# Row dot products and softmax: x of a batch loaded as one 8 MB transfer instead of two of 4 MB

## Chip, cores and metric

One Trainium2 chip, one core. The metric is the device time of one execution in microseconds (us). Executions of the kernel before ran from 325.33 to 326.04 us (0.2%), so a difference of 1 us (0.3%) needs several runs, and one of 0.5 us needs the trace as well. Every run also has a span: the time from the program's first instruction to the end of its last. It is about 2 us shorter than the device time.

## What the kernel must compute

```python
B, N, D = 8, 4096, 512          # x, y: float32 [B, N, D]
gram = np.matmul(x, y.transpose(0, 2, 1))
diag = np.diagonal(gram, axis1=1, axis2=2)      # diag[b, n] = sum over d of x[b, n, d] * y[b, n, d]
diag = diag - diag.max(axis=-1, keepdims=True)
exp = np.exp(diag)
out = exp / exp.sum(axis=-1, keepdims=True)     # [8, 4096]
```

Only the diagonal is needed, so the work is 32,768 dot products of 512 elements and a softmax per batch. Each input byte is used once: x and y are 134.22 MB, and all of it must come from memory.

Of the kernel before, what the change touches and what calls it, by code (L numbers as in the profile page):

```python
# [1 line left out]

# [5 lines left out]


@with_exitstack
def kernel(
    ctx: ExitStack,
    tc: tile.TileContext,
    x: bass.AP,
    y: bass.AP,
    out: bass.AP,
):
    nc = tc.nc
    f32 = mybir.dt.float32  # L20
    B, N, D = x.shape
    P = nc.NUM_PARTITIONS
    R = N // P
    H = R // 2


    xv = x.rearrange("b (p r) d -> b p r d", p=P)
    yv = y.rearrange("b (p r) d -> b p r d", p=P)
    ov = out.rearrange("b (p r) -> b p r", p=P)

    io = ctx.enter_context(tc.tile_pool(name="io", bufs=3))
    persist = ctx.enter_context(tc.tile_pool(name="persist", bufs=1))
    sm = ctx.enter_context(tc.tile_pool(name="sm", bufs=2))

    diag = persist.tile([P, B * R], f32, name="diag")
    res = persist.tile([P, B * R], f32, name="res")

    def load(b, r0, parts):
        xt = io.tile([P, H, D], f32, tag="xt", name="xt")
        yt = io.tile([P, H, D], f32, tag="yt", name="yt")  # L40
        o = 0
        for n in parts:
            nc.sync.dma_start(out=xt[:, o : o + n, :], in_=xv[b, :, r0 + o : r0 + o + n, :])  # L43
            nc.sync.dma_start(out=yt[:, o : o + n, :], in_=yv[b, :, r0 + o : r0 + o + n, :])
            o += n
        return xt, yt

    def dots(b, r0, xt, yt):
        for k in range(H):
            c = b * R + r0 + k  # L50
            nc.vector.scalar_tensor_tensor(  # L51
                out=xt[:, k, :],
                in0=xt[:, k, :],
                scalar=1.0,
                in1=yt[:, k, :],
                op0=mybir.AluOpType.mult,
                op1=mybir.AluOpType.mult,
                accum_out=diag[:, c : c + 1],
            )

    def softmax(b):
        db = diag[:, b * R : (b + 1) * R]
        rb = res[:, b * R : (b + 1) * R]
        mxp = sm.tile([P, 1], f32, tag="mxp", name="mxp")
        nc.vector.tensor_reduce(out=mxp, in_=db, axis=mybir.AxisListType.X, op=mybir.AluOpType.max)  # L65
        mx = sm.tile([P, 1], f32, tag="mx", name="mx")
        nc.gpsimd.partition_all_reduce(out_ap=mx, in_ap=mxp, channels=P, reduce_op=bass_isa.ReduceOp.max)  # L67
        nmx = sm.tile([P, 1], f32, tag="nmx", name="nmx")
        nc.vector.tensor_single_scalar(out=nmx, in_=mx, scalar=-1.0, op=mybir.AluOpType.mult)  # L69
        sump = sm.tile([P, 1], f32, tag="sump", name="sump")  # L70
        nc.scalar.activation(  # L71
            out=rb, in_=db, func=mybir.ActivationFunctionType.Exp,
            bias=nmx, scale=1.0, accum_out=sump,
        )
        ssum = sm.tile([P, 1], f32, tag="ssum", name="ssum")
        nc.gpsimd.partition_all_reduce(out_ap=ssum, in_ap=sump, channels=P, reduce_op=bass_isa.ReduceOp.add)  # L76
        rc = sm.tile([P, 1], f32, tag="rc", name="rc")
        nc.vector.reciprocal(out=rc, in_=ssum)  # L78
        nc.vector.tensor_single_scalar(out=rb, in_=rb, scalar=rc, op=mybir.AluOpType.mult)  # L79
        nc.scalar.dma_start(out=ov[b], in_=rb)  # L80

    for b in range(B):
        for h in range(2):
            last = b == B - 1 and h == 1
            parts = [8, 4, 2, 1, 1] if last else [H]
            xt, yt = load(b, h * H, parts)
            dots(b, h * H, xt, yt)
        softmax(b)


# [1 line left out]
_INS = ['x', 'y']  # L92
_OUTS = [((8, 4096), 'float32')]


# [23 lines left out]
```

## The kernel before

Partition p holds rows 32p to 32p+31 of a batch, so its rows are one contiguous run of 64 KB in memory. A batch is worked in two halves of 16 rows. Each half has an x tile and a y tile of 32 KB per partition, in three buffers each (192 KB per partition in all).

```python
R = N // P        # 32 rows per partition
H = R // 2        # 16
io = ctx.enter_context(tc.tile_pool(name="io", bufs=3))
...
def load(b, r0, parts):
    xt = io.tile([P, H, D], f32, tag="xt", name="xt")
    yt = io.tile([P, H, D], f32, tag="yt", name="yt")
    o = 0
    for n in parts:
        nc.sync.dma_start(out=xt[:, o : o + n, :], in_=xv[b, :, r0 + o : r0 + o + n, :])
        nc.sync.dma_start(out=yt[:, o : o + n, :], in_=yv[b, :, r0 + o : r0 + o + n, :])
        o += n
    return xt, yt

def dots(b, r0, xt, yt):
    for k in range(H):
        c = b * R + r0 + k
        nc.vector.scalar_tensor_tensor(out=xt[:, k, :], in0=xt[:, k, :], scalar=1.0, in1=yt[:, k, :],
            op0=mult, op1=mult, accum_out=diag[:, c : c + 1])
...                      # softmax(b): two reductions over partitions, one exp, one store
for b in range(B):
    for h in range(2):
        last = b == B - 1 and h == 1
        parts = [8, 4, 2, 1, 1] if last else [H]
        xt, yt = load(b, h * H, parts)
        dots(b, h * H, xt, yt)
    softmax(b)
```

The last half comes in pieces of 8, 4, 2, 1 and 1 rows, so that little work is left when the last byte lands.

## Time and profile before

| | before |
|---|---|
| time, median | 325.55 us (3 runs, 325.4 to 325.62) |
| span in the profile | 323.8 us |
| load packets, time per DMA engine (sum over packet records / 16) | 313.0 us |
| 32 KB packet | 1213 ns (median) |
| last load landed | 318.36 us |
| middle of its 16 parts landed; 15 of the 16 landed | 314.60 us; 314.83 us |

Lines of the page of the kernel before: busy time of the engines, and part 3, which has for each DMA queue its packets, megabytes and the share of the span of 16 DMA engines that its packets took. The load queue fills 96.6% of the DMA engines' time; VectorE (DVE) only half of its own. "q14 instruction" is the queue that fetches the engines' instructions, five packets within the span.

```profile
span 323.8 us, 727 instructions
DVE 164.4 (51%) x544; ACT 4.6 (1%) x17; POOL 6.1 (2%) x20
...
q1 hardware_dynamic: 5760, 134.22, 96.6%
q10 hardware_dynamic: 1152, 0.13, 0.3%
q14 instruction: 5, 0.04, 0.0%
```

The same kernel by stretches of time. After the stretch come the busy times of the engines, the granted clock, the mean share of the DMA engines that was busy, and the rate. From 22 to 306 us the DMA engines have no free time (share 1.00, 431 GB/s). From 306 to 318 us the share falls to 0.70 although the last load lands only at 318.36 us: most DMA engines are done and wait for one.

```profile
core 0: us, DVE busy (x) ACT busy (x) POOL busy (x), PEclk, DMA share, GB/s
22.00:306.00 284.00, 151.07 (x501) 2.90 (x14) 5.13 (x14) 1.00 1.00 431
306.00:318.00 12.00, 11.87 (x40) 0.00 (x0) 0.00 (x0) 1.00 0.70 279
```

The groups of the page (line, engine, operation, count, busy us, mean ns, then the idle time of the engine before them and what ended it), and the end of the chain of waits (start, length, what). All waits of VectorE's products are for loads of y (in the softmaxes it waits another 11.9 us for GpSimd); after the last landing there are about 5.5 us of products, softmax and store.

```profile
L51 DVE SCALAR_TENSOR_TENSOR xt<-xt,yt 128x512 f32<-128x512 f32 x256 | 158.3, 687 | 144.1 <-DMA yt<-in_y_dram 144.1
```

```profile
269.00 39.28 DMA yt<-in_y_dram
308.28 0.01 issue
308.30 10.06 DMA yt<-in_y_dram
...
318.45 0.71 DVE xt L51 x2
...
321.31 0.24 DVE res L79
```

### The profile page before, as it was taken

The page shows a single profiled execution, that of the slowest core. Times are in us where ns is not written, and L with a number is a line of the kernel's source. Part 1 is how long each engine was busy: PE and PEld are TensorE (multiplying, and loading weights), DVE is VectorE, ACT ScalarE, POOL GpSimd, SP SyncE. Part 2 cuts the span into 40 slices and gives each one's busy share as a digit, 9 for nine tenths or more (in the row PEclk, how much of TensorE's full clock was granted, in tenths as well). Part 3 has the DMA queues.
Part 4 walks back from the last instruction along what each step waited for, and adds up shares of the span by engine and source line. Part 5 has one row for each costly group of instructions (what it writes and reads, how often), then busy time and mean ns, then how long its engine had stood idle before and what let it go on. Part 6 is the DMA issues. An engine that isn't in the chain of part 4 may idle for free.

```text
span 323.8 us, 727 instructions
## 1 busy us (share of the span) xinstructions
DVE 164.4 (51%) x544; ACT 4.6 (1%) x17; POOL 6.1 (2%) x20
## 2 busy tenths in 40 slices
DVE  0019075290944709256191742908348091571994
ACT  1000000000000000000000000000000000000000
POOL 0000000000000000000000000000000000000000
DMA  8999999999999999999999999999999999999980
GB/s 324 453 401 441 453 410 429 455 409 433 449 397 451 445 401 446 450 398 449 449 397 450 452 393 453 445 397 455 445 397 453 446 394 453 445 397 425 429 319 10
DMA packets 6917, 134.39 MB, mean 415 GB/s; under 512 B 1792, under 2 KB 1792, under 8 KB 2560
## 3 DMA queue, kind: packets, MB, share of 16 engines
q1 hardware_dynamic: 5760, 134.22, 96.6%
q10 hardware_dynamic: 1152, 0.13, 0.3%
q14 instruction: 5, 0.04, 0.0%
HBM read 134.22 MB, written 0.13 MB: 415 GB/s over the span
## 4 chain that ended last, share of the span: by engine, by line
DMA 82%; DVE 16%; issue 1%; SPq 0%; POOLq 0%; POOL 0%; DVEq 0%
DMA yt<-in_y_dram 82%; DVE xt L51 16%; SPq L43 0%; DVE mxp L65 0%; POOLq L114 0%; POOL mx L67 0%; DVE res L79 0%; DVE rc L78 0%; DVEq L51 0%; DVEq L79 0%; POOLq L67 0%
## 5 line engine op out<-in xcount | busy, mean ns | idle before, releaser
L51 DVE SCALAR_TENSOR_TENSOR xt<-xt,yt 128x512 f32<-128x512 f32 x256 | 158.3, 687 | 144.1 <-DMA yt<-in_y_dram 144.1
L51 DVE DVE_READ_ACCUMULATOR xt<-xt,yt 128x1 f32 x256 | 21.1, 82 | 0.0
L67 POOL PARTITION_ALL_REDUCE mx<-mxp x8 | 2.8, 350 | 308.9 <-DVE mxp L65 308.9
L71 ACT ACTIVATE res<-diag,nmx 128x32 f32<-128x32 f32 x8 | 2.6, 321 | 315.2 <-DVE nmx L69 315.2
L78 DVE RECIPROCAL rc<-ssum 128x1 f32<-128x1 f32 x8 | 1.3, 164 | 7.6 <-POOL ssum L76 7.6
L69 DVE TENSOR_SCALAR nmx<-mx 128x1 f32<-128x1 f32 x8 | 1.2, 154 | 4.3 <-POOL mx L67 4.3
L76 POOL PARTITION_ALL_REDUCE ssum<-sump x8 | 3.1, 383 | 5.8 <-ACT res L71 5.8
L79 DVE TENSOR_SCALAR res<-res,rc 128x32 f32<-128x32 f32 x8 | 1.9, 241 | 0.9
L65 DVE TENSOR_REDUCE mxp<-diag 128x1 f32<-128x32 f32 x8 | 1.5, 186 | 0.3
L71 ACT ACTIVATION_READ_ACCUMULATOR res<-diag,nmx 128x1 f32 x8 | 1.5, 186 | 0.0
L71 ACT ACT_TABLE_LOAD x1 | 1.3, 1283 | 0.7 <-PEq L103 0.7
L103 POOL MEMSET const-float32-0.0<- 128x1 f32 x1 | 0.1, 98 | 0.2 <-issue 0.2
L103 POOL MEMSET const-bfloat16-1.0<- 128x1 bf16 x1 | 0.1, 102 | 0.0
L103 POOL MEMSET const-uint8-127<- 128x1 uint8 x1 | 0.1, 101 | 0.0
L103 POOL MEMSET const-float32-1.0<- 128x1 f32 x1 | 0.1, 98 | 0.0
## 6 DMA issues: line engine op xcount, KB each, us to landing
xt<-in_x_dram SPq DMA_DIRECT2D x15, 4096.0 KB, 39.6
yt<-in_y_dram SPq DMA_DIRECT2D x15, 4096.0 KB, 48.9
xt<-in_x_dram SPq DMA_DIRECT2D x1, 2048.0 KB, 34.7
yt<-in_y_dram SPq DMA_DIRECT2D x1, 2048.0 KB, 39.3
xt<-in_x_dram SPq DMA_DIRECT2D x1, 1024.0 KB, 41.3
yt<-in_y_dram SPq DMA_DIRECT2D x1, 1024.0 KB, 43.4
xt<-in_x_dram SPq DMA_DIRECT2D x1, 512.0 KB, 35.5
yt<-in_y_dram SPq DMA_DIRECT2D x1, 512.0 KB, 27.0
```

The source lines that it names most:

```text
L51: nc.vector.scalar_tensor_tensor(out=xt[:, k, :], in0=xt[:, k, :], scalar=1.0, in1=yt[:, k, :], op0=mybir.AluOpType.mult, op1=mybir.AluOpT ...
L65: nc.vector.tensor_reduce(out=mxp, in_=db, axis=mybir.AxisListType.X, op=mybir.AluOpType.max)
L67: nc.gpsimd.partition_all_reduce(out_ap=mx, in_ap=mxp, channels=P, reduce_op=bass_isa.ReduceOp.max)
L69: nc.vector.tensor_single_scalar(out=nmx, in_=mx, scalar=-1.0, op=mybir.AluOpType.mult)
L71: nc.scalar.activation(out=rb, in_=db, func=mybir.ActivationFunctionType.Exp, bias=nmx, scale=1.0, accum_out=sump,)
L76: nc.gpsimd.partition_all_reduce(out_ap=ssum, in_ap=sump, channels=P, reduce_op=bass_isa.ReduceOp.add)
L78: nc.vector.reciprocal(out=rc, in_=ssum)
L79: nc.vector.tensor_single_scalar(out=rb, in_=rb, scalar=rc, op=mybir.AluOpType.mult)
L103: nc = _bacc.Bacc("TRN2", target_bir_lowering=False, num_devices=1)
```

## The change

The intent: larger transfers and longer runs. x of a whole batch comes in one 8 MB load (64 KB per partition, two buffers), y in two halves (32 KB per partition, two buffers), again 192 KB. The products are written over y instead of x. The last batch keeps halves and pieces.

```diff
-    io = ctx.enter_context(tc.tile_pool(name="io", bufs=3))
+    io = ctx.enter_context(tc.tile_pool(name="io", bufs=2))
...
+    def load_x(b, xt, r0, n):
+        nc.sync.dma_start(out=xt[:, r0 : r0 + n, :], in_=xv[b, :, r0 : r0 + n, :])
+    def load_y(b, yt, r0, o, n):
+        nc.sync.dma_start(out=yt[:, o : o + n, :], in_=yv[b, :, r0 + o : r0 + o + n, :])
...
-                out=xt[:, k, :],
-                in0=xt[:, k, :],
+                out=yt[:, k, :],
+                in0=xt[:, r0 + k, :],
...
     for b in range(B):
+        last = b == B - 1
+        xt = io.tile([P, R, D], f32, tag="xt", name="xt")
+        if not last:
+            load_x(b, xt, 0, R)
         for h in range(2):
-            last = b == B - 1 and h == 1
-            parts = [8, 4, 2, 1, 1] if last else [H]
-            xt, yt = load(b, h * H, parts)
+            yt = io.tile([P, H, D], f32, tag="yt", name="yt")
+            o = 0
+            for n in [8, 4, 2, 1, 1] if last and h == 1 else [H]:
+                if last:
+                    load_x(b, xt, h * H + o, n)
+                load_y(b, yt, h * H, o, n)
+                o += n
             dots(b, h * H, xt, yt)
```

More of the change, by code (lines that the diff above doesn't have):

```diff
@@ L36 @@
     res = persist.tile([P, B * R], f32, name="res")
-    def load(b, r0, parts):
-        xt = io.tile([P, H, D], f32, tag="xt", name="xt")
-        yt = io.tile([P, H, D], f32, tag="yt", name="yt")
-        o = 0
-        for n in parts:
-            nc.sync.dma_start(out=xt[:, o : o + n, :], in_=xv[b, :, r0 + o : r0 + o + n, :])
-            nc.sync.dma_start(out=yt[:, o : o + n, :], in_=yv[b, :, r0 + o : r0 + o + n, :])
-            o += n
-        return xt, yt
+    def load_x(b, xt, r0, n):
+        nc.sync.dma_start(out=xt[:, r0 : r0 + n, :], in_=xv[b, :, r0 : r0 + n, :])
+    def load_y(b, yt, r0, o, n):
+        nc.sync.dma_start(out=yt[:, o : o + n, :], in_=yv[b, :, r0 + o : r0 + o + n, :])
     def dots(b, r0, xt, yt):
```

## The prediction

> **What bounds the kernel now.** The DMA engines. The page gives 134.22 MB on the load queue, 96.6% of 16 engines' span of 323.8 us; the table by stretch of time gives DMA share 1.00 and 431 GB/s from 22 to 306 us. The trace's packet records show 1213 ns (median) per 32 KB packet, 432 GB/s for 16 engines. The Trainium skill (DMA: Bandwidth & Descriptors, "Where 436 GB/s comes from") puts the ceiling at 435 GB/s; this trace agrees. VectorE is busy 51%; its waits are all for y loads (144.1 us). A load lands 39 to 49 us after its issue, while one 4 MB load takes 9.7 us (landings at 12.9, 22.6, 32.3, 42.0), so the queue is never empty.
>
> The span: 1.74 us to the first packet; 313.0 us of load packets per engine; 0.9 us of output packets; then one engine finishes late. The 16 landings of the last load spread over 3.84 us, 15 of them close together. The late engine falls back about 1 us at each of four instruction fetches on queue 14 (8 KB, at 47, 125, 186 and 263 us), about every 130 VectorE instructions. The same page ("Queues, rings and completion order") calls row 14 the runtime's, refill among its uses. From the last landing (318.36 us) 5.4 us of products, softmax and store follow.
>
> **What the change does.**
> - Bytes: unchanged. This is the bound.
> - Packets: in 7 of 8 batches two 32 KB runs of x become one of 64 KB, if one packet may carry that. Packets of 2, 4, 8, 16, 32 KB take 86, 160, 312, 611, 1213 ns: 602 ns per 16 KB plus 9 ns. Seven batches x 128 packets fewer are 56 per engine: 0.5 us. If the run is cut into 32 KB packets, nothing.
> - DMAs: 7 fewer, each one completion packet of 9 ns per engine: 0.06 us.
> - VectorE: the same 256 products (687 ns, 613 ns apart), in place in y instead of x; about 7 fewer semaphore waits. Off the critical path; the four fetches stay.
> - Buffers: the same 192 KB per partition. A y half is issued when the products of the same half of the batch before are done, about 10.4 us after that half landed. By then the queue holds at least 17 us more (rest of y, 19.4 us of x): no starvation. The lead was about 28 us.
> - The last batch: the same halves and pieces, so the tail of 5.4 us stays, and the wait for the late engine.
>
> **On the critical path:** only 0.5 to 0.6 us of packet overhead. Larger transfers buy almost nothing, because 32 KB packets already pay under 1% each.
>
> **Prediction:** 325.0 us (325.55 - 0.55), 80% range 323.9 to 326.2. Chances: faster by over 2% 0.01, within 2% 0.98, slower by over 2% 0.01.
>
> **What would show it.** Right: load packets of 64 KB near 2417 ns; about 896 fewer packets; DMA share 1.00 through the middle; no gap between loads; the last landing about 0.5 us earlier, its spread still near 4 us; tail 5.4 us. Wrong: 64 KB packets slower or faster than twice 1213 ns; gaps where y waits for VectorE; another count or cost of queue 14 fetches.
>
> **What would make it wrong.** A fetch could cost the late engine more when it meets a 64 KB packet (up to 1 us for each of four); or the fetches cost less or fall differently, and the late engine catches up (up to 3.7 us less). A starved queue would need VectorE or the issue to lag by 17 us.

## The result

| | before | after |
|---|---|---|
| time, median of 4 runs | 325.52 us | 325.14 us |
| range | 325.4 to 325.62 | 325.1 to 325.49 |
| ratio, 95% interval | | 0.9991 [0.9974, 1.0008] |

A ratio is the mean time of one kernel's fast runs over the mean of the other's in the same rounds, so it is not quite the ratio of the medians quoted. The interval holds 1.

The spans are sharper than the times. Over nine runs of the changed kernel (here and in after_again) they are 323.0 to 323.5 us, over 34 runs of the kernel before in all rounds with experiments 323.6 to 324.3 us: no overlap.

The page after, the same lines. 1008 packets fewer are on the load queue: 896 of them because two runs of 32 KB became one of 64 KB, and 112 completion packets of the 7 loads that are gone (16 each). The share of the DMA engines' time is the same 96.6% of a span that is 0.7 us shorter.

```profile
span 323.1 us, 714 instructions
DVE 163.9 (51%) x544; ACT 4.6 (1%) x17; POOL 6.1 (2%) x20
...
q1 hardware_dynamic: 4752, 134.22, 96.6%
q10 hardware_dynamic: 1152, 0.13, 0.3%
q14 instruction: 4, 0.03, 0.0%
```

By stretches of time: still 1.00 through the middle, still a fall before 318 us.

```profile
core 0: us, DVE busy (x) ACT busy (x) POOL busy (x), PEclk, DMA share, GB/s
22.00:306.00 284.00, 151.40 (x503) 2.90 (x14) 5.16 (x14) 1.00 1.00 432
306.00:318.00 12.00, 11.42 (x37) 0.00 (x0) 0.00 (x0) 1.00 0.65 258
```

VectorE's group, and the end of the chain. VectorE waits as long as before (143.8 us), and the last landing is at 317.58 us instead of 318.36.

```profile
L47 DVE SCALAR_TENSOR_TENSOR yt<-xt,yt 128x512 f32<-128x512 f32 x256 | 157.9, 687 | 143.8 <-DMA yt<-in_y_dram 143.8
```

```profile
288.19 19.32 DMA yt<-in_y_dram
307.51 0.02 issue
307.52 10.06 DMA yt<-in_y_dram
...
317.68 0.71 DVE yt L47 x2
...
320.54 0.24 DVE res L75
```

From the packet records: a 64 KB packet takes 2419 ns (median), a 32 KB packet 1213 ns, so the rate is the same.

**The late DMA engine.** Each load lands in 16 parts, read here as one per DMA engine. These are landing times of six loads in each kernel, read from the trace (us: first part, middle part, last part, spread):

```
before  51.26  51.51  52.52  1.27      after   70.52  70.83  71.56  1.05
        80.48  80.68  81.71  1.22             109.33 109.62 110.36  1.03
       148.65 148.77 150.71  2.06             148.13 148.43 150.16  2.03
       197.26 197.35 200.28  3.02             254.78 255.14 257.84  3.06
       265.31 265.41 269.32  4.01             305.97 306.29 310.00  4.03
       314.52 314.60 318.36  3.84             313.71 314.02 317.58  3.87
```

In the last line of each, 15 of the 16 parts land close together and one alone, about 3.5 us later. The spread grows in steps of about 1 us, and each step follows a packet of queue 14. These are the packet records around the first step of the kernel before (start ns, duration ns, end ns, bytes, queue; cut):

```
47420  1221  48641  32768   1
47438   332  47770   8192  14
47439  1213  48652  32768   1
...
47758  1875  49633  32768   1
```

After the instruction packet the next packet of one engine takes 1875 ns instead of 1213. Every fetch while loads run has exactly one such packet behind it, in six of the traces that were gone through for it: 1787 to 1875 ns for one of 32 KB, 2948 to 3081 ns instead of 2419 for one of 64 KB. So the prediction's worry that a fetch costs more when it meets a 64 KB packet is settled: the loss is about 0.6 us either way, besides the fetch's own 0.3 us. (The records carry no engine number; that it is always the same engine is read from one landing standing alone.) The packets come at 47.4, 125.0, 185.5 and 263.0 us before, and at 48.3, 122.0, 195.8 and 272.0 us after.

### The profile page after: what moved, and what is told of

Its sections match the earlier page's. It is cut to its first block, busy times and chain, and to the rows that moved or that the text cites. A ratio compares the mean times of both kernels' runs of the same rounds, so it can differ in the third digit from the quotient of the medians.

```text
span 323.1 us, 714 instructions
## 1 busy us (share of the span) xinstructions
DVE 163.9 (51%) x544; ACT 4.6 (1%) x17; POOL 6.1 (2%) x20
## 3 DMA queue, kind: packets, MB, share of 16 engines
q1 hardware_dynamic: 4752, 134.22, 96.6%
## 4 chain that ended last, share of the span: by engine, by line
DMA 73%; DVE 25%; issue 1%; POOLq 0%; SPq 0%; POOL 0%; DVEq 0%
DMA yt<-in_y_dram 73%; DVE yt L47 25%; POOLq L118 0%; SPq L39 0%; POOL mx L63 0%; DVE res L75 0%; DVE mxp L61 0%; DVE rc L74 0%; DVEq L47 0%; DVEq L75 0%; POOLq L63 0%
## 5 line engine op out<-in xcount | busy, mean ns | idle before, releaser
L47 DVE SCALAR_TENSOR_TENSOR yt<-xt,yt 128x512 f32<-128x512 f32 x256 | 157.9, 687 | 143.8 <-DMA yt<-in_y_dram 143.8
L47 DVE DVE_READ_ACCUMULATOR yt<-xt,yt 128x1 f32 x256 | 21.0, 82 | 0.0
```

Source lines behind the costliest of these rows:

```text
L47: nc.vector.scalar_tensor_tensor(out=yt[:, k, :], in0=xt[:, r0 + k, :], scalar=1.0, in1=yt[:, k, :], op0=mybir.AluOpType.mult, op1=mybir.A ...
```

## The experiments

One table from the traces: instruction fetches while loads run, the landing of the middle part of the last load (most engines are done), the landing of its last part, the difference, and the median time.

| kernel | fetches | most done, us | last, us | late by, us | time, us |
|---|---|---|---|---|---|
| before | 4 | 314.60 | 318.36 | 3.76 | 325.52 |
| after | 4 | 314.02 | 317.58 | 3.56 | 325.14 |
| after_again | 4 | 314.28 | 317.65 | 3.37 | 325.37 |
| x_two_loads | 4 | 314.94 | 318.58 | 3.64 | 325.57 |
| before_two_bufs | 4 | 314.41 | 318.38 | 3.97 | 325.54 |
| runs_8k | 4 | 320.81 | 324.80 | 3.99 | 332.34 |
| runs_2k | 4 | 345.41 | 349.16 | 3.75 | 356.55 |
| more_instr | 6 | 313.96 | 319.58 | 5.62 | 326.89 |
| few_instr | 1 | 317.44 | 318.01 | 0.57 | 328.74 |
| few_instr2 | 1 | 314.83 | 317.00 | 2.17 | 323.95 |
| few_instr3 | 1 | 314.14 | 314.89 | 0.75 | 322.37 |
| before_few_instr | 1 | 314.61 | 315.51 | 0.90 | 322.74 |
| before_few_again | 1 | 314.40 | 315.56 | 1.16 | 322.81 |

The theory (A): the stream of packets through 16 DMA engines is the bound; a packet costs a few ns over its bytes, so the change can gain half a microsecond; and the end waits for one engine that instruction fetches have put behind. All kernels below gave a correct result.

### after_again: the changed kernel once more

> The changed kernel once more, timed five times against before on one chip, so that the next three have it beside them. Theory A (the stream of packets through 16 DMA engines is the bound, a packet costs about 9 ns over its bytes, and the last landing waits for one engine that instruction fetches have put behind): 0.4 to 0.8 us under before, about 325.1 us, last load landing at 317.6 us, its 16 landings spread over 3.9 us. Rival B (the change does nothing, the 0.4 us of the first result are noise): the interval holds 1.000 and the median is within 0.2 us of before.

Measured: 325.37 us (5 runs, 325.05 to 325.66) against 325.63 us of before (9 runs); ratio 0.9990 [0.9976, 1.0003]. Last landing 317.65 us, spread 3.50 us. The trace repeats the earlier landing (0.7 us before that of the old kernel). In time, the difference of the medians is 0.26 us; both intervals hold 1. That is less than the 0.4 to 0.8 us of theory A, and outside the 0.2 us of rival B too. So the times alone don't establish the gain.

The spans do: 323.32 us against 323.93 us in the mean of these rounds, 0.61 us less. In the changed kernel 2.0 us of the time lies outside the span, in the kernel before 1.8 us, so a third of the gain is not in the device time. One thing goes with this: in after, after_again, runs_8k and runs_2k the last instruction fetch comes after the span's end (at 324.89 us in after; in the kernel before at 322.72 us, inside it), and these have 1.96 to 2.05 us outside the span in the mean; all others, whose trace has no fetch there, have 1.77 to 1.82 us. That the fetch causes it was not tested.

### x_two_loads: all of the change but the 64 KB runs

```diff
         if not last:
-            load_x(b, xt, 0, R)
+            load_x(b, xt, 0, H)
+            load_x(b, xt, H, H)
```

> Everything of the change but the 64 KB runs: the 8 MB tile of x is filled by two 4 MB loads of 32 KB runs. Theory A: 896 packets more, 56 per engine at about 9 ns, so 0.5 us over the changed kernel and equal to before within 0.2 us; last landing near 318.1 us. Rival B: equal to the changed kernel within 0.2 us. Rival C (it is the order of the loads or the buffers that moved the 0.8 us of the landing): last landing stays at 317.6 us though the packets are 32 KB.

Measured: 325.57 us (5 runs), ratio to before 0.9998 [0.9985, 1.0011]; last landing 318.58 us. With the 32 KB packets back, the landing is near that of the kernel before, and so is the time; so it is not the order of loads that moved it (rival C). The landing is 0.5 us later than expected, in a run that was the slowest of its five. The difference from after_again in time, 0.2 us, is under what the rounds resolve, and just where rival B put it; the mean spans of the same rounds, 323.88 against 323.32 us, speak against rival B.

One more reading of the traces leaves out the late engine and the end. From the middle landing of the last y load of batch 0 to that of batch 6 it takes 233.25 to 233.73 us in the five traces with 32 KB runs of x (before, before_two_bufs, x_two_loads, before_few_instr, before_few_again; mean 233.40), and 232.82 to 233.18 us in the six with 64 KB (after, after_again, more_instr, the three few_instr kernels; mean 233.02). Six batches gain 0.4 us. Theory A, with the 8 ns found below for each of 8 packets and 9 ns for a completion packet, gives 0.44 us.

### before_two_bufs: the buffers alone

```diff
-    io = ctx.enter_context(tc.tile_pool(name="io", bufs=3))
+    io = ctx.enter_context(tc.tile_pool(name="io", bufs=2))
```

> The kernel before with two buffers of each half instead of three, nothing else: the lead of the loads over the products falls from about 28 us to about 7 us (one pair of 19.4 us in the queue less 12.4 us from a landing to the next packets that its products release). Theory A: the queue is still never empty, so 325.5 us, equal to before within 0.3 us. Rival F (the third buffer is worth something, so the change gained more in packets than shows and lost it in buffers): slower than before by 0.5 us or more, with gaps between loads.

Measured: 325.54 us against 325.53 us, ratio 0.9999 [0.9984, 1.0014]. As expected: with fused products the third buffer is worth nothing, and no loss in the buffers hid a gain of the change.

### runs_8k and runs_2k: the packet cost made large

Both pad the tiles, so that the same loads are cut into shorter runs (runs_2k has `G = 1`; the indices of the products follow):

```diff
+    G = 4
+    PAD = 8
+    xg = x.rearrange("b (p r g) d -> b p r (g d)", p=P, g=G)
...
-        nc.sync.dma_start(out=xt[:, r0 : r0 + n, :], in_=xv[b, :, r0 : r0 + n, :])
+        if n >= G:
+            nc.sync.dma_start(out=xt[:, r0 // G : (r0 + n) // G, : G * D], in_=xg[b, :, r0 // G : (r0 + n) // G, :])
...
-        xt = io.tile([P, R, D], f32, tag="xt", name="xt")
+        xt = io.tile([P, R // G, G * D + PAD], f32, tag="xt", name="xt")
```

> The changed kernel with 32 bytes of padding after every four rows in the tiles, so that the same loads, of the same bytes, are cut into runs of 8 KB. Theory A: 1008 packets of 8 KB per engine at 313 ns each, 322 us of packets per engine instead of 312.2, so 9.8 us more: 335.0 us (+3.0%). Rival G (the bound is the bytes alone, and a packet's own cost hides behind the next packet): 325.1 us.

> The same with padding after every row: runs of 2 KB. Theory A: 4096 packets per engine at 86 to 87 ns each, 352 to 358 us of packets, so 40 to 45 us more than the changed kernel: 365 to 370 us (+12 to 14%). Rival G: 325.1 us.

Measured: 332.34 us (ratio 1.0205 [1.0190, 1.0220]) and 356.55 us (ratio 1.0950 [1.0931, 1.0968]), both clearly slower. The direction holds and rival G falls, but the sizes were too large: 7.0 us over the changed kernel instead of 9.8, and 31.2 us instead of 40 to 45. The failed step of these two expectations is the sum of packet durations. The page of runs_2k shows it: more than all of the engines' time.

```profile
span 354.7 us, 714 instructions
...
DMA packets 67220, 134.38 MB, mean 379 GB/s; under 512 B 1680, under 2 KB 1680, under 8 KB 67216
...
q1 hardware_dynamic: 66064, 134.22, 101.2%
```

A packet's record must then overlap that of the next on the same engine by some ns, so durations may not be added for short packets. The step from packet to packet comes from landings instead. In runs_2k two y loads of 128 packets per engine land 10.69 us apart, less 9 ns for the completion packet: 83.4 ns a packet (its record says 86). In runs_8k, 32 packets in 9.87 us less 9 ns: about 308 ns. In before, 8 packets in 9.71 us less 9 ns: 1212.6 ns. The three lie within about 1 ns of one line, 37.64 ns per KB plus about 8 ns. So 56 packets fewer per engine are worth 0.45 us, and with 7 completion packets of 9 ns, 0.5 us. The prediction's 9 ns, taken from durations, was a little high, which matters little for 56 packets and much for 3832 (runs_2k has 4096 load packets per engine, the changed kernel 264).

### more_instr: two more fetches

```diff
             dots(b, h * H, xt, yt)
+            if not last:
+                for _ in range(17):
+                    nc.vector.memset(junk, 0.0)
```

> The changed kernel with 17 VectorE memsets of 128x1 after each half of batches 0 to 6: 238 VectorE instructions more that do nothing for the result, VectorE still waiting for data. Theory A: two more instruction fetches in the stream (six instead of four), each putting one engine about 0.97 us further behind: spread 5.9 us instead of 3.9 us, last landing near 319.5 us, time about 327.1 us (1.9 us over the changed kernel). Rival D: unchanged, 325.1 us.

Measured: 326.89 us (5 runs), ratio to before 1.0040 [1.0028, 1.0053]; 1.5 us over after_again in time (expected 1.9), 1.9 us in the mean span. The built program ran most of the memsets at the start, where VectorE waits for the first load, so fetches came already at 12 and 26 us; there were six in all, as expected. Most engines finish when they did (313.96 us), and the late one 5.62 us after them. In the profiled runs the last landing is 1.9 to 2.0 us later than in the changed kernel. Two fetches, 1 us each: rival D falls, since nothing else about the loads changed. The lines of the page:

```profile
span 325.1 us, 952 instructions
...
q14 instruction: 6, 0.05, 0.0%
```

### few_instr: fewer instructions, and what it broke

```diff
-            dots(b, h * H, xt, yt)
+            if last:
+                dots(b, h * H, xt, yt)
+            else:
+                c = b * R + h * H
+                nc.vector.tensor_tensor(out=yt, in0=xt[:, h * H : h * H + H, :], in1=yt, op=mybir.AluOpType.mult)
+                nc.vector.tensor_reduce(out=diag[:, c : c + H], in_=yt, axis=mybir.AxisListType.X, op=mybir.AluOpType.add)
```

> The changed kernel, but in batches 0 to 6 VectorE does each half in one multiplication of 128x8192 and one sum over rows of 512, instead of 16 fused products with 16 accumulator reads: about 160 VectorE instructions instead of 571. VectorE works longer (about 17 us per half instead of 9.9, still under the 19.4 us in which a half of x and y arrives). Theory A: at most one instruction fetch within the stream instead of four; the spread of the 16 landings of the last load falls from 3.9 us to 1.5 us or less; last landing near 314.1 to 315.1 us, time 321.6 to 322.6 us, 2.5 to 3.5 us under the changed kernel. Rival D (the late engine is slow for another reason, such as its memory addresses or its ports, and the fetches only coincide): spread and time stay, 325.1 us. Rival E (VectorE's load matters): slower, because VectorE is now busy over 80%.

Measured: 328.74 us (4 runs), ratio 1.0093 [1.0079, 1.0107]: slower by 0.9%, as rival E (VectorE's load matters) had it. One fetch, and the late engine is only 0.57 us late, as expected of A. But two new costs came, both because a half now holds its buffer for 17.4 us. The timeline of few_instr (start, length, engine, line, operation) shows that the y load of 300.21 us had to wait for the products of batch 6:

```profile
282.89 0.33 SPq L42 DMA_DIRECT2D yt<-in_y_dram  x1
283.27 0.42 SPq L39 DMA_DIRECT2D xt<-in_x_dram  x1
291.49 8.69 DVE L98 TENSOR_REDUCE diag<-yt 128x16 f32<-128x8192 f32 x1
300.21 0.33 SPq L42 DMA_DIRECT2D yt<-in_y_dram  x1
```

By stretches of time, the DMA engines have a hole there (share 0.67 from 296 to 302 us, about 2 us):

```profile
280.00:296.00 16.00, 15.96 (x3) 0.00 (x0) 0.00 (x0) 1.00 0.99 416
296.00:302.00 6.00, 4.52 (x3) 0.41 (x2) 0.70 (x2) 1.00 0.67 249
302.00:318.00 16.00, 15.83 (x53) 0.00 (x0) 0.03 (x1) 1.00 0.93 379
```

And VectorE enters the last batch with a backlog: at the last landing (318.01 us) products remain until 322.2 us. The late engine's 3 us were won and more than 6 us lost. I had compared VectorE's 17 us with the 19.4 us of a half's data, and not asked how long the buffer is held or what remains at the end. The prediction had missed this too: it gives the queue 17 us of lead when a y half is issued. The trace of the changed kernel has 16.3 to 18.8 us there in batches 1 to 6, but only 6.8 us for the first y half of the last batch (issued at 277.51 us, the x load ahead of it lands at 284.27), because x comes in halves there, and 10.8 us for the load behind it that waits for a half. In few_instr these two are issued 5.4 and 12.0 us later.

### few_instr2: the backlog taken away

```diff
-            if last:
+            if last or (b == B - 2 and h == 1):
                 dots(b, h * H, xt, yt)
```

> As few_instr, but the second half of batch 6 goes back to the 16 fused products (9.9 us instead of 17.4), so that the buffers it holds come free before the queue runs dry and VectorE has no backlog at the end; about 181 VectorE instructions. Theory A: one fetch in the stream, no hole in the DMA near 297 us, spread of the last 16 landings about 0.8 us, most engines finish near 314.2 us as in the changed kernel, last landing near 314.9 us, tail 5.5 us, time about 322.5 us: 2.7 to 3.0 us under the changed kernel, 3.0 us (0.9%) under before. Rival D (few fetches and a small spread, but the time was not the late engine's to give): 325 us or more even without the hole and the backlog.

Measured: 323.95 us (6 runs, 322.96 to 325.05), ratio 0.9947 [0.9929, 0.9965]. Faster by 0.5%, but 1.4 us short of the expectation, with runs scattered by 2 us and the last engine 2.17 us late. The y load that waits for the first half of batch 6 was issued at 282.94 us; the load ahead of it had its last packets at 283.7 to 284.5 us. On most engines the first packets after it took 1.6 to 2.1 us instead of 1.21 (as the second packets at the start of the kernel before, 1.4 to 2.1 us), and one engine then had a packet of 2.16 us. The stretch of few_instr2 there:

```profile
283.00:286.00 3.00, 3.00 (x11) 0.00 (x0) 0.00 (x0) 1.00 0.83 295
```

### few_instr3: the same half released 3.5 us earlier

```diff
                 c = b * R + h * H
+                m = H // 2 if b == B - 2 else H
...              # multiplication and sum over rows 0 to m of the half
+                dots(b, h * H, xt, yt, m)          # rows m to 16 as fused products
```

> As few_instr2, but the first half of batch 6 is done as 8 rows in one multiplication and one sum and 8 rows as fused products, 13.7 us instead of 17.4. In few_instr2 the load that waits for this half was issued at 282.9 us, while the load ahead of it in the queue ended at 283.7 to 284.5 us; here it should be issued near 279.2 us, 4.5 us ahead. Theory H (what few_instr2 lost against its expectation is that queue running dry in the shorter lead of two buffers: packets of 1.6 to 2.1 us on the restart and one engine 1 us further behind): no slow packets near 284 us, spread 1.1 us or less, the runs within 0.5 us of each other, time 322.0 to 322.8 us. Rival I (a layout with 64 KB packets loses the time to the late engine in another way): spread about 2.5 us and runs scattered by 2 us again, 323.5 us or more.

Measured: 322.37 us (4 runs, 322.19 to 322.6), ratio 0.9905 [0.9889, 0.9922]. The load was issued at 279.42 us, the packets near 284 us take 1213 to 1222 ns, the last engine is 0.75 us late, and the scatter is 0.4 us. Theory H holds: few_instr2 had let its queue run dry. (The first packets after the gap start at 283.90 us, 0.95 us after the issue.) The same stretch of few_instr3:

```profile
283.00:286.00 3.00, 3.00 (x11) 0.00 (x0) 0.00 (x0) 1.00 0.94 404
```

A second fetch came at 316.2 us, after the last load, and cost no load anything.

### before_few_instr and before_few_again: the same idea without the change

```diff
-            dots(b, h * H, xt, yt)
+            if b == B - 1:
+                dots(b, h * H, xt, yt)
+            else:
+                c = b * R + h * H
+                nc.vector.tensor_tensor(out=xt, in0=xt, in1=yt, op=mybir.AluOpType.mult)
+                nc.vector.tensor_reduce(out=diag[:, c : c + H], in_=xt, axis=mybir.AxisListType.X, op=mybir.AluOpType.add)
```

> The kernel before (32 KB runs, three buffers), with one multiplication and one sum per half in batches 0 to 6, about 160 VectorE instructions. Theory A: the gain is independent of the change under study: one fetch instead of four, spread about 0.9 us or less, most engines done near 314.6 us, last landing near 315.4 us, time about 322.9 us, 2.6 us under before and within 0.5 us of few_instr2. The third buffer keeps the queue full without the exception for batch 6. Rival: if the 64 KB runs matter once the late engine is out of the way, few_instr2 is faster than this by more than 0.6 us.

> The same kernel as before_few_instr, on the chip of few_instr3, as its measure. Theory A: 322.7 us again, and few_instr3 0.2 to 0.7 us faster, which is the packets' share of the change (0.4 to 0.8 us at the last landing of the earlier runs). Rival B (64 KB packets are worth nothing): equal within 0.2 us.

The page of before_few_instr, for the fetches and VectorE's load:

```profile
span 321.0 us, 312 instructions
DVE 268.5 (84%) x124; ACT 4.6 (1%) x17; POOL 6.1 (2%) x20
...
q14 instruction: 1, 0.01, 0.0%
```

Measured: 322.74 us (4 runs), ratio 0.9911 [0.9899, 0.9924]; and again 322.81 us (4 runs), ratio 0.9916 [0.9901, 0.9930], on the chip of few_instr3. So the gain of fewer fetches does not need the change, and three buffers carry it without any exception for batch 6. (The expectation of 0.5 us or less from few_instr2 was missed by that kernel's dry queue: 1.2 us.) few_instr3 is 0.44 us faster than this (medians, same rounds), within the expected 0.2 to 0.7. But in the profiled runs, which are 0.64 us apart, only 0.26 us is in the time at which most engines are done; the rest is how late the last engine is (0.75 against 1.16 us). The two ratios' intervals overlap. How much of the 0.44 us the 64 KB packets give stays open.

## Why the prediction was right

- **The bound.** Right. The DMA engines moved 431 to 432 GB/s with no free time from 22 to 306 us in both kernels. The bytes did not change.
- **Packets.** Right: 896 fewer, 64 KB packets at 2419 ns (predicted 2417), a gain of 0.5 us in the sum worked out from them (0.4 us over six batches between landings; the added-up records fell by 0.76 and 0.46 us in the two traces). The cost per packet from landings is 8 ns, not the 9 ns of the durations; for 56 packets that is 0.06 us. runs_8k and runs_2k show the size of the term where it matters.
- **The size in time.** Predicted 325.0, measured 325.14 and 325.37. The times can't tell this from no change at all, which also lies in the range of 323.9 to 326.2 us; the spans, 0.6 us shorter, and the landings can. The last landing came 0.7 to 0.8 us earlier, slightly more than the 0.5 to 0.6; the time at which most engines are done differs by 0.3 us between two runs of the same kernel (314.02 and 314.28 us), so the excess lies within that scatter.
- **No starvation.** Right in its outcome: VectorE's wait and the DMA share did not change, and the kernel before with two buffers is as fast. But the margin was stated too large: the lead was 6.8 us, not 17, at the last batch, and it was all but consumed when VectorE took 7.5 us longer for a half (few_instr, few_instr2). The changed kernel, with two buffers, is the less forgiving one.
- **The late engine.** Right: four fetches while loads run, a spread of 3.87 us at the last load. more_instr showed that fetches cause it, and few_instr3 and before_few_instr that it is on the critical path: about 3 us of the time went with three of the four fetches.
- **The tail.** Predicted 5.4 us; 323.1 - 317.58 = 5.5 us, the same 5.5 us as before (323.84 - 318.36).

## What to carry to other kernels

When the DMA engines are full and packets are already 32 KB, a longer run can save only the few ns per packet that it removes: count the packets per engine before rebuilding the buffers. Look at the 16 landings of the last load, too: a single engine that is late sets the end, and here it was the instruction stream of a half-idle VectorE that made it late, so 16 small instructions replaced by two large ones gained 0.9% where the change under study gained about 0.1% in time (0.2% in the span). When instructions become longer, recompute how long each buffer is held and whether the next load is still issued before the queue runs dry.

## What the Trainium skill lacked or had wrong

- Runtime: NRT & Kernel Launch, "Instruction fetch mechanics", gives refills of 16 KiB blocks (256 instructions) and calls their cost mostly hidden. Here the refills were single 8 KB packets, one per about 128 VectorE instructions (at counts 54, 180, 306 and 438 of VectorE's records in the changed kernel). VectorE shows no wait for them, but each put one of the 16 saturated DMA engines about 1 us behind, 3.4 to 4.0 us at the last load for four of them.
- DMA: Bandwidth & Descriptors, "Queues, rings and completion order", names refill as a use of row 14; the traces agree, but no page read here says what an 8 KB refill costs a full engine: a packet of 309 to 333 ns, and the next 32 KB packet 1787 to 1875 ns instead of 1213.
- DMA: Bandwidth & Descriptors, "Where 436 GB/s comes from": 435 GB/s as the ceiling of the fabric. The traces agree, 432 GB/s with 32 KB packets. The same section says, with no condition, that for transfers between HBM and SBUF about 358 GB/s of the HBM side binds; these loads from HBM, with one core running, moved 431 to 432 GB/s for 284 us.
- No page read here has the cost of letting a full load queue run dry: first packets of 1.6 to 2.1 us instead of 1.21, and one engine a further 1 us behind (few_instr2).
